# Mixers' modulation weights multiplied on POOL and summed on ACT, with inputs in one transfer, tables on POOL and the ones products reordered

## The chip, the cores and the metric

The kernel runs on one core of a Trainium2 chip. The metric is the device time of one execution in microseconds (us); of the kernel before three runs gave a median of 806.41 us (806.21 to 808.29). The engines are PE (TensorE), DVE (VectorE), ACT (ScalarE), POOL (GpSimd) and SP, whose queue issues the transfers.

## The reference

Two layers of a trunk on x (256 tokens x 1024 channels, f32), each a mixer and a convolutional FFN, both behind a modulated RMSNorm; a last RMSNorm ends it.

```python
for l in range(2):
    mod = c @ mod_w[l] + mod_b[l]                     # 1024 -> 6 x 1024
    sh1, sc1, g1, sh2, sc2, g2 = split(mod, 6)
    h = rmsnorm(x, norm1_g[l]) * (1 + sc1) + sh1
    x = x + g1 * mixer(h, positions, w_in[l], ...)    # sparse + forgetting attention, gates, w_out
    h = rmsnorm(x, norm2_g[l]) * (1 + sc2) + sh2
    x = x + g2 * conv_ffn(h, w_up[l], conv_w[l], conv_b[l], w_down[l])
return rmsnorm(x, final_g)
```

All is f32. The mixer's index branch picks the 64 best keys of each query, and both attentions have 8 heads of 64.

## The kernel before, in words

Channels lie on partitions: x is a tile of 128 x 8 x 256 (eight blocks of 128 channels, 256 tokens). To keep f32 accuracy at the speed of one pass, every weight chunk of 128 x 1024 (0.5 MB) is split into a rounded part `whi` (ACT, line 202) and the rest `wlo` (DVE, line 214, two inputs in SBUF), the activations into `hh` and `hl`, and each product is three matmuls (`mm3`, line 121).

Work is a list of steps (`add`, line 133), each with the weight chunks that it takes; `run_steps` (line 141) issues the loads on SP's queue into a ring of six slots (`RAW`), splits ahead by up to five (`SPLIT`), and calls the step. Engines named in `pin(...)` keep program order; the scheduler of the framework may reorder the others. A slot is loaded again once its last reader is done, and SP's queue keeps order.

The stages, with their place in the profiled execution: the start and the first mixer's row projection (0 to 52 us, `begin` to `go`, lines 566 to 676), the rest of mixer 0 (to 214), FFN 0 (to 405), mixer 1 (to 594), FFN 1 (to 787) and the end (`last`, `tail`, `finish`, lines 1094 to 1159).

Modulation vectors come in two ways. For layer 0's first two (shift and scale of the first norm) PE does it: `mod_mm` (line 615) multiplies chunks `wmod` by c, `mod_fin` (line 626) turns the sum, and `h_block` makes the next block of h; this runs once per block k, in front of the row products of k, with four PE transposes and small DVE steps in between. All others go through `mod_columns` (line 348): one DVE instruction per chunk of 128 x 1024 multiplies by `cB` (c broadcast) and sums (TENSOR_TENSOR_REDUCE, shown as CUSTOM_DVE_ANT_0), with the bias as its start value. There are 80: 24 in mixer 0 (`MIXV[0]`), 16 in mixer 1 and 40 in the FFNs, of which 32 are in FFN 0. In the mixers one such chunk goes with each bulk weight chunk (`bulk`, line 753).

The norms' sums go through PE: squares from ACT, partly added on DVE (`sq_add`, the first `DSUM` = 4 blocks), are multiplied by a column of ones (`sum_rows`, line 381); `rstd` (line 386) does the power on POOL, and `rstd_rows` spreads it over partitions on PE. `warm` (line 588) issues products that nobody reads, which keep PE busy while it waits there (`WARMS`).

At the start five transfers bring positions, frequencies, vectors and x (lines 245 to 250). Masks and rotary tables (`masks`, `tables`, lines 290 and 303) are 32 small, mostly DVE instructions between the squares of x.

Of the kernel before, what the change touches and what calls it, by code (L numbers as in the profile page):

```python
# [16 lines left out]
P = 128  # L17
# [22 lines left out]
WARMS = {"ffn": (4, 8, 10), "mixer": (0, 8, 7)}  # L40
# [9 lines left out]
DSUM = 4  # L50
# [15 lines left out]


@with_exitstack
def hybrid_trunk(ctx: ExitStack, tc: tile.TileContext, xT, vec, fbias, pos, invf,
# [39 lines left out]
    pad(const, 48)  # L109
# [147 lines left out]
    V.tensor_scalar(ident, jp, 0.0, None, op0=OP.is_equal)  # L257
    tri = const.tile([P, 3 * P], F32, name="tri")
    V.memset(tri[:, 0:P], 0.0)
    V.memset(tri[:, 2 * P:], 1.0)  # L260
    causal = const.tile([P, T], F32, name="causal")
    V.memset(causal[:, 0:P], 0.0)
    chunked = const.tile([P, T], F32, name="chunked")
    V.memset(chunked, 0.0)
    V.memset(chunked[0:64, P + 64:], NEG)
# [12 lines left out]
    V.tensor_copy(cpad[:, :, 0], vc[:, V_C:V_C + KT])  # L278
    cB = const.tile([P, D], F32, name="cB")
    LF = const.tile([P, 2, P], F32, name="LF")  # L280
    V.memset(LF, 0.0)
    cum = const.tile([P, T], F32R, name="cum")
    V.memset(f(cum), 0.0)
# [6 lines left out]
    def masks():  # L290
        V.tensor_scalar(tri[:, P:2 * P], jp, 0.0, None, op0=OP.is_ge)
        V.tensor_scalar(causal[:, P:], jp, 0.0, NEG, op0=OP.is_gt, op1=OP.mult)
        V.tensor_scalar(e0, ph, 0.0, -8.0, op0=OP.is_equal, op1=OP.mult)
        V.tensor_scalar(e1, ph, 32.0, -8.0, op0=OP.is_equal, op1=OP.mult)
        V.tensor_add(e2, e0, e1)
        V.tensor_copy(pick, e2)
# [6 lines left out]
    def tables():  # L303

        posf = const.tile([P, 2], F32, name="posf")
        V.tensor_copy(posf, posi)
        ang = const.tile([P, 2, 8], F32, name="ang")
        for j in range(2):
            V.tensor_scalar(ang[:, j, :], ivf, posf[:, j:j + 1], None, op0=OP.mult)
# [15 lines left out]
        V.tensor_scalar(nt, ang, PI, -TWO_PI, op0=OP.is_gt, op1=OP.mult)
        V.tensor_add(ang, ang, nt)
        V.tensor_scalar(nt, ang, -PI, TWO_PI, op0=OP.is_lt, op1=OP.mult)
        V.tensor_add(ang, ang, nt)
        V.tensor_scalar(ang, ang, 3.1415925, -3.1415925, op0=OP.min, op1=OP.max)
        A.activation(ss[:, :, 8:16], ang, AF.Sin)  # L330
        V.scalar_tensor_tensor(nt, ang, -1.0, ang, op0=OP.mult, op1=OP.min)
        V.tensor_scalar(nt, nt, PI / 2, None, op0=OP.add)
# [15 lines left out]
    def mod_columns(l, v, kind=("m",)):  # L348

        def part(n, raw):  # L350
# [6 lines left out]
            if kind[0] == "s":  # L357
                pin()
        return [((lambda raw, n=n: part(n, raw), (wmodT[COLS.index((l, v)), n], D, *kind)), None)
                for n in range(KT)]  # L360

# [203 lines left out]

    def begin():
        sq = work.tile([P, 2, 4, T], F32, name="sq0", tag="hl")
        ACC["s"] = []
# [6 lines left out]
        a, b = ACC["s"]  # L575
        V.tensor_add(a, a, b)
# [7 lines left out]
    add(tables, ahead=0)  # L584
    add(masks, ahead=0)
    HH = {}

    def warm(n):

        if n:  # L590
            t = bank("M")
        for _ in range(n):
            PE.matmul(t[:, :T], cum[:, :P], cum, start=True, stop=True)

    def mixer(l, tail=None, sums=None):
        S = {}

        def start():
            HH["h"] = work.tile([P, KT, T], F32R, name="hh"), work.tile([P, KT, T], F32R, name="hl")
            S["idx"] = [[bank("A") for _ in range(2)] for _ in range(2)]  # L600
            S["fox"] = [halves(bank("B")) for _ in range(2)]
# [12 lines left out]
        if l == 0:  # L614
# [27 lines left out]
            def go0(a, b):  # L642
                pin("V", "A", "PE")
                start()
                mod_mm(0, 0, a)
                sp = bank("C")
                sum_rows(sp, ACC["s"][0], True, True)
                mod_mm(0, 1, b)
                r = rstd(sp)
                state["split_hi"](1)  # L650
                mod_fin(0, r)
            add(go0, *mchunks[0], ahead=0)

            def go(k, w, *mc):
                hh, hl = HH["h"]
                if k == 0:
                    mod_both(1, *mc[:2])
                    mc = mc[2:]
                if k + 1 == KT:
# [3 lines left out]
                    clear_keys()  # L663
                    return
                state["split_hi"](2)
# [5 lines left out]
                if mc:  # L671
                    mod_both(k + 2, *mc)
            for k in range(KT):
                add(lambda *c, k=k: go(k, *c), (wrow[l, k], 1096, "w"),
                    *(mchunks[1] if k == 0 else ()), *(mchunks[k + 2] if k + 2 < KT else ()), ahead=0 if k + 1 < KT else None)
            add(rest)
        else:
# [7 lines left out]
            def second():  # L685
                warm(WARMS["mixer"][1])
                S["rb"] = rstd_rows(r=S["r"])
                warm(WARMS["mixer"][2])
# [19 lines left out]
            def go(k, w):  # L708
# [7 lines left out]
                if k == 1:  # L716
                    pin()
            for k in range(KT):
# [505 lines left out]
```

## Time and profile before

| | |
|---|---|
| median of 3 runs | 806.41 us (806.21 to 808.29) |
| the profiled execution, its own time | 800.14 us |
| its span, first to last instruction | 798.3 us |
| PE busy | 774.5 us (97%), 6419 matmuls |
| DVE busy | 671.2 us (84%) |
| ACT busy | 486.8 us (61%) |
| POOL busy | 8.0 us (1%) |
| DMA | 179.7 MB, 225 GB/s in the mean |

A share of the span is a mean over stages with different limits, so the view of busy time by stretch is the one to read, cut at the stages' ends. Matmuls are pipelined: a busy PE may still issue at different paces, which shows in the count of matmuls per stretch. Instructions that all go through a helper have line 88; they are told apart by their tiles.

### The profile page before, as it was taken

How to read it: one execution, taken by the hardware profiler on the slowest of the kernel's cores; microseconds unless marked ns; L12 is line 12 of the kernel's file. 1: busy time of each engine (PE TensorE's matmuls, PEld its weight loads, DVE VectorE, ACT ScalarE, POOL GpSimd, SP SyncE). 2: the span in 40 equal slices, each digit the busy share in tenths (PEclk: the TensorE clock that was granted, in tenths of full speed). 3: DMA queues.
4: the chain of work that ended last, by engine and by line, in shares of the span. 5: the costliest groups of instructions: out<-in, count | busy, mean ns of one | idle time of the engine just before them, and what ended most of it. 6: DMA issues, size and time to landing. Idle time of an engine off the chain costs nothing.

```text
span 798.3 us, 16595 instructions
## 1 busy us (share of the span) xinstructions
PE 774.5 (97%) x6419; PEld 749.7 (94%) x6419; DVE 671.2 (84%) x1441; ACT 486.8 (61%) x888; POOL 8.0 (1%) x21
## 2 busy tenths in 40 slices
PE   4999999999999999999999999999999999999996
PEld 2899989989999999999989999999999999999996
DVE  6689999998589999998776899997858887877764
ACT  4476566655386665667555756675538666666664
POOL 2000000000000000000000000000000000000000
PEclk9999999999999999999999999999999999999998
DMA  8956777888558999977534577784755766556501
GB/s 324 407 177 204 259 231 255 281 291 289 191 161 285 331 337 334 330 243 225 170 120 122 161 249 248 245 283 150 240 195 156 257 218 211 188 185 186 185 27 54
DMA packets 51919, 179.74 MB, mean 225 GB/s; under 512 B 6272, under 2 KB 6400, under 8 KB 51840
## 3 DMA queue, kind: packets, MB, share of 16 engines
q1 hardware_dynamic: 51840, 178.68, 66.5%
q8 instruction: 50, 0.82, 0.4%
q14 instruction: 29, 0.24, 0.1%
HBM read 177.61 MB, written 1.05 MB: 224 GB/s over the span
## 4 chain that ended last, share of the span: by engine, by line
PE 62%; issue 26%; DVE 8%; ACT 3%; DMA 1%; SPq 0%; POOLq 0%; POOL 0%; DVEq 0%; ACTq 0%
PE psA L88 39%; PE psB L88 19%; DVE wlo L88 2%; PE psM L88 2%; DVE sc L88 1%; PE psC L88 1%; DVE raw L88 1%; ACT whi L88 1%; DMA raw<-wqkf 1%; DMA x<-xT 1%; DVE lg L88 1%; DVE m L88 0%; ACT sq L88 0%; ACT y L88 0%; DVE x L88 0%
## 5 line engine op out<-in xcount | busy, mean ns | idle before, releaser
L88 ACT ACTIVATE whi<-raw 128x1024 fp32r<-128x1024 f32 (+3 forms) x252 | 254.3, 1013 | 140.8 <-PE psA L88 55.8
L88 DVE TENSOR_TENSOR wlo<-raw,whi 128x1024 fp32r<-128x1024 f32 (+3 forms) x252 | 292.1, 1165 | 56.3 <-ACT whi L88 55.4
L88 PE MATMUL psB<-hl,whi 128*128 128x256 f32 x768 | 212.9, 279 | 0.5 <-DVE hl L88 0.5
L88 PE MATMUL psB<-hh,whi 128*128 128x256 f32 x768 | 212.8, 279 | 0.0
L88 PE MATMUL psB<-hh,wlo 128*128 128x256 f32 x768 | 212.6, 278 | 0.0
L88 PEld LDWEIGHTS psB<-hl,whi 128*128 128x128 f32 x768 | 143.7, 188 | 1.0 <-DVE hl L88 0.9
L88 PEld LDWEIGHTS psB<-hh,wlo 128*128 128x128 f32 x768 | 144.0, 188 | 0.0
L88 PEld LDWEIGHTS psB<-hh,whi 128*128 128x128 f32 x768 | 143.6, 188 | 0.2
L88 PE MATMUL psA<-hh,whi 128*128 128x256 f32 x448 | 127.7, 286 | 0.1
L88 PE MATMUL psA<-hl,whi 128*128 128x256 f32 x448 | 125.3, 280 | 0.0
L88 PE MATMUL psA<-hh,wlo 128*128 128x256 f32 x448 | 125.0, 280 | 0.0
L88 DVE CUSTOM_DVE_ANT_0 raw<-raw,cB,vc 128x1024 f32<-128x1024 f32 x80 | 101.6, 1272 | 0.5 <-DMA raw<-wmodT 0.5
L88 PE MATMUL psA<-gl,whi 128*128 128x256 f32 x352 | 97.7, 278 | 0.0
L88 PE MATMUL psA<-gh,whi 128*128 128x256 f32 x352 | 97.4, 279 | 0.3
L88 PE MATMUL psA<-gh,wlo 128*128 128x256 f32 x352 | 97.6, 278 | 0.0
L88 PEld LDWEIGHTS psA<-hh,whi 128*128 128x128 f32 x448 | 84.0, 188 | 2.2 <-issue 1.7
L88 PEld LDWEIGHTS psA<-hl,whi 128*128 128x128 f32 x448 | 84.2, 188 | 0.4
L88 PEld LDWEIGHTS psA<-hh,wlo 128*128 128x128 f32 x448 | 84.1, 188 | 0.0
L88 DVE SCALAR_TENSOR_TENSOR y<-us,vc,y 128x255 f32<-128x255 f32 (+1 forms) x176 | 76.1, 477 | 3.8 <-ACT y L88 3.7
L88 PEld LDWEIGHTS psA<-gh,whi 128*128 128x128 f32 x352 | 65.7, 188 | 0.7 <-ACT gh L88 0.7
L88 PEld LDWEIGHTS psA<-gh,wlo 128*128 128x128 f32 x352 | 66.2, 188 | 0.0
L88 PEld LDWEIGHTS psA<-gl,whi 128*128 128x128 f32 x352 | 66.0, 188 | 0.0
(202 smaller groups left out, 1173.5 us busy)
## 6 DMA issues: line engine op xcount, KB each, us to landing
raw<-wup SPq DMA_DIRECT2D x88, 512.0 KB, 4.3
raw<-wmodT SPq DMA_DIRECT2D x80, 512.0 KB, 4.9
raw<-wdn SPq DMA_DIRECT2D x44, 512.0 KB, 3.9
raw<-wgate SPq DMA_DIRECT2D x32, 512.0 KB, 4.5
raw<-wrow SPq DMA_DIRECT2D x16, 548.0 KB, 6.5
raw<-wbr SPq DMA_DIRECT2D x16, 512.0 KB, 4.8
raw<-wout SPq DMA_DIRECT2D x16, 512.0 KB, 4.0
raw<-wqa SPq DMA_DIRECT2D x16, 320.0 KB, 2.9
```

The lines of the kernel that those rows point to most:

```text
L88: r = fn(*a, **kw)
```

## The change

POOL multiplies each of the mixers' 40 modulation chunks by `cB` in place, and ACT sums it (Identity with an accumulator); DVE adds the bias once per vector. In mixer 1 six of the 16 chunks go into the row steps k = 2 to 7. The inputs that the start needs go in front of x in one array, which two transfers bring. Constant tiles, masks and the angles of the rotary tables are made on POOL in pieces between the first row steps; `clear_keys` goes from the last row step to the start. Products that nobody reads run on PE from the start (`warm`; the old `warm` is now `idle`). The sums of squares of the two halves of x go through PE one by one, and the row products of block 0 are issued in three passes around the modulation of block 1. Chunks for `mod_mm` are taken one block ahead instead of two. `gains` of the second norm moves into the last `merge`; the split behind FFN's first blocks and the opening of its modulation loads (`epoch`) go from block 1 to block 4. At the FFNs' ends fewer squares are added on DVE (3 and 2 instead of 4), the last one's sums go between its blocks, and the result leaves in two transfers instead of four.

```diff
-WARMS = {"ffn": (4, 8, 10), "mixer": (0, 8, 7)}
+WARMS = {"ffn": (4, 8, 10), "mixer": (3, 9, 7)}
-DSUM = 4
+DSUM = (3, 2)
+NS = 96
-    pad(const, 48)
+    pad(const, 80)
-    nc.sync.dma_start(posi, pos)
-    nc.sync.dma_start(ivf, invf)
-    nc.sync.dma_start(vc[:, :V_L + V_CW], vec[:, :V_L + V_CW])
-    for i in range(2):
-        nc.sync.dma_start(x[:, 4 * i:4 * i + 4, :], xT[:, 4 * i:4 * i + 4, :])
+    nc.sync.dma_start(xs[:, :half], xT[:, :half])
+    nc.sync.dma_start(xs[:, half:], xT[:, half:])
...
-    V.memset(f(cum), 0.0)
+    G.memset(f(cum), 0.0)
...
+    def mod_products(vectors):
+        def part(l, v, n, raw):
+            raw = raw[:, :D]
+            G.tensor_tensor(raw, raw, cB, op=OP.mult)
+            A.activation(raw, raw, AF.Identity, accum_out=MOD[l][:, 8 * v + n:8 * v + n + 1])
+            if n == KT - 1:
+                o = V_L + l * V_PER + V_MODB + 8 * v
+                m = MOD[l][:, 8 * v:8 * v + 8]
+                V.tensor_tensor(m, m, vc[:, o:o + 8], op=OP.add)
...
+    def warm(n):
+        for _ in range(n):
+            PE.matmul(HD["fox"][1][:, 0, :], cum[:, :P], cum, start=True, stop=True, skip_group_check=True)
     def begin():
+        pin("V", "PE")
+        clear_keys()
+        HD["fox"] = [halves(bank("B")) for _ in range(2)]
+        HD["sp"] = bank("C")
+        warm(20)
...
+        V.tensor_scalar(ident, jp, 0.0, None, op0=OP.is_equal)
+        G.tensor_copy(cpad[:, :, 0], xs[:, V_C:V_C + KT])
+        G.tensor_copy(vc[:, :V_L + V_CW], xs[:, :V_L + V_CW])
...
-        a, b = ACC["s"]
-        V.tensor_add(a, a, b)
...
             def go0(a, b):
                 pin("V", "A", "PE")
+                sum_rows(HD["sp"], ACC["s"][0], True, False)
+                mod_mm(0, 0, a)
+                sum_rows(HD["sp"], ACC["s"][1], False, True)
+                r = rstd(HD["sp"])
+                mod_mm(0, 1, b)
+                state["split_hi"](1)
+                warm(4)
+                mod_fin(0, r)
+                warm(10)
                 start()
...
+            def first(w, a, b):
+                products(w, 0)
+                state["split_hi"](2)
+                mod_both(1, a, b)
+                products(w, 1)
+                state["split"](2)
+                mod_fin(1)
+                products(w, 2)
...
+                for fn in {0: [masks, angles], 1: [turns, clamp], 3: [tables]}.get(k, ()):
+                    add(fn, ahead=0)
...
+            late += mod_products(MIXV[l])
             for k in range(KT):
                 add(lambda w, k=k: go(k, w), (wrow[l, k], 1096, "w"), ahead=(0, 0, 1)[k] if k < 3 else None)
+                if k > 1:
+                    m, keep = late.pop(0)
+                    add(*m, keep=keep)
...
-        for v in MIXV[l]:
-            mods += mod_columns(*v)
+        mods += late
...
-                if k == 1:
+                if k == 4:
                     state["split"](4)
                     epoch(l + 1)
                     pin()
...
-                    if n < DSUM:
+                    if n < DSUM[l]:
...
+                if l + 1 == L:
+                    if b == 2:
+                        sum_rows(S["sp"], ACC["a"], True, False)
+                        pin("A", "PE")
+                    while sq and sq[0][0] < 2 * b:
+                        sums(False)
...
+            A.activation(y[:, 0, c], S["tok"][i][0], AF.Copy, scale=r[:, 0:1])
+            V.tensor_scalar(y[:, 1, c], S["tok"][i][1], r[:, 1:2], None, op0=OP.mult)
+            nc.sync.dma_start(rows[:, :, c], y[:, :, c])
```

## Rows read from the trace of the kernel before

**Rows 1.** Stretches: us; busy PE, PEld, DVE, ACT, POOL (count); clock; DMA share; GB/s.

```profile
17.60:49.90 32.30, 32.17 (x291) 27.61 (x287) 19.73 (x44) 15.19 (x23) 0.00 (x0) 1.00 0.87 337
...
88.00:180.00 92.00, 89.72 (x723) 84.02 (x722) 90.31 (x253) 58.34 (x144) 0.00 (x0) 1.00 0.80 270
...
240.00:400.00 160.00, 160.00 (x1414) 160.00 (x1413) 151.36 (x245) 102.96 (x158) 0.00 (x0) 1.00 0.82 281
...
469.00:538.00 69.00, 68.58 (x546) 64.16 (x546) 68.05 (x205) 46.40 (x119) 0.00 (x0) 1.00 0.79 265
...
640.00:780.00 140.00, 140.00 (x1191) 140.00 (x1190) 104.45 (x161) 88.22 (x133) 0.00 (x0) 1.00 0.53 170
...
5.00:17.60 12.60, 6.44 (x42) 3.21 (x42) 8.37 (x40) 5.61 (x8) 0.81 (x2) 1.00 1.02 406
...
405.00:409.10 4.10, 4.10 (x22) 3.97 (x21) 1.15 (x4) 1.10 (x3) 0.69 (x1) 0.58 0.01 4
```

**Rows 2.** Timeline of the start: start us, us, engine, line, what, idle before.

```profile
2.11 0.91 SPq L250 DMA_DIRECT2D x<-xT  x2
...
7.92 1.06 ACT L88 ACTIVATE sq<-x 128x1024 f32<-128x1024 f32 x1 [0.23 <-DMA x<-xT]
...
15.74 1.94 PE L88 MATMUL psM<-raw,cpad 128*32 128x256 f32 x16
...
17.60 0.64 PE L88 MATMUL psA<-whi,hh 128*128 128x320 f32 x1
...
21.93 1.07 PE L88 MATMUL psM<-rawg,cpad 128*32 128x256 f32 x16
...
22.93 0.54 PE L88 MATMUL psA<-whi,hh 128*128 128x320 f32 x2
```

**Rows 3.** Groups by line in 88 to 180 us: shapes, count, busy us, mean ns.

```profile
L88 DVE CUSTOM_DVE_ANT_0 raw<-raw,cB,vc 128x1024 f32<-128x1024 f32 x24 | 30.4, 1272 | 0.5 <-DMA raw<-wmodT 0.5
L88 DVE TENSOR_TENSOR wlo<-raw,whi 128x1024 fp32r<-128x1024 f32 (+1 forms) x24 | 28.8, 1200 | 0.4 <-ACT whi L88 0.4
L88 ACT ACTIVATE whi<-raw 128x1024 fp32r<-128x1024 f32 x24 | 25.4, 1060 | 22.1 <-PE psA L88 15.6 <-DMA raw<-wgate 4.8 <-DMA raw<-wqkf 1.4
...
L88 DVE TENSOR_SCALAR lg<-lg,rs 128x128 f32<-128x128 f32 (+1 forms) x32 | 8.8, 314 | 0.0
...
L88 ACT ACTIVATION_READ_ACCUMULATOR lg<-lg,nb 128x1 f32 x32 | 6.1, 192 | 0.0
```

**Rows 4.** Waits of PE over the whole span: us, times, longest.

```profile
PE psA L88 <- DVE lg L88: 2.5, 3, 1.2
```

**Rows 5.** Timeline of the start: POOL's memsets and small DVE instructions beside and behind them.

```profile
3.56 0.55 POOL L301 MEMSET kzl<- 128x512 f32 x1
...
4.18 0.47 DVE L88 CAST ri<-nt 128x16 int32<-128x16 f32 x1
...
5.38 0.17 DVE L88 CAST ri<-nh 128x16 int32<-128x16 f32 x1
```

**Rows 6.** Timeline where FFN 0 and mixer 1 begin: from the variance to h.

```profile
216.43 0.16 DVE L88 TENSOR_SCALAR var<-psC 128x2 f32<-128x2 f32 x1 [1.13 <-PE psC L88]
...
218.16 0.87 DVE L88 SCALAR_TENSOR_TENSOR ht<-x,gain,psC 128x256 f32<-128x256 f32 x2 [1.58 <-PE psC L88]
...
405.23 0.16 DVE L88 TENSOR_SCALAR var<-psC 128x2 f32<-128x2 f32 x1 [1.24 <-PE psC L88]
...
407.92 0.87 DVE L88 SCALAR_TENSOR_TENSOR ht<-x,gain,psC 128x256 f32<-128x256 f32 x2 [2.53 <-PE psC L88]
```

**Rows 7.** Timeline of the end.

```profile
787.48 0.42 DVE L88 TENSOR_TENSOR sqacc<-sqacc,sq 128x256 f32<-128x256 f32 x1 [0.48 <-ACT sq L88]
...
787.82 1.65 DVE L88 SCALAR_TENSOR_TENSOR x<-psA,mod,x 128x256 f32<-128x256 f32 x4
...
790.21 0.40 ACT L88 ACTIVATE sq<-x 128x256 f32<-128x256 f32 x1
...
793.42 1.82 SPq L1159 DMA_DIRECT2D out_dram<-yout  x4
```

More of the change, by code (lines that the diff above doesn't have):

```diff
@@ L583, in hybrid_trunk, with idle @@
     add(begin, ahead=0)
-    add(tables, ahead=0)
-    add(masks, ahead=0)
     HH = {}
-    def warm(n):
+    def idle(n):
         if n:
@@ L598, in start @@
         def start():
-            HH["h"] = work.tile([P, KT, T], F32R, name="hh"), work.tile([P, KT, T], F32R, name="hl")
+            if "sp" not in HD:
+                HH["h"] = work.tile([P, KT, T], F32R, name="hh"), work.tile([P, KT, T], F32R, name="hl")
+            HD.pop("sp", None)
             S["idx"] = [[bank("A") for _ in range(2)] for _ in range(2)]
-            S["fox"] = [halves(bank("B")) for _ in range(2)]
+            S["fox"] = HD.pop("fox", None) or [halves(bank("B")) for _ in range(2)]
+        late = []
+        if l == 0:
+            late += mod_products(MIXV[l])
         def rows(k, w, part):
@@ L643, in go0, with products @@
                 pin("V", "A", "PE")
-                start()
[L645 to L651, printed above, removed]
-            add(go0, *mchunks[0], ahead=0)
+                sum_rows(HD["sp"], ACC["s"][0], True, False)
[5 more added lines that the diff above has]
+                warm(4)
+                HH["h"] = work.tile([P, KT, T], F32R, name="hh"), work.tile([P, KT, T], F32R, name="hl")
+                mod_fin(0, r)
+                warm(10)
+                start()
+            add(go0, *mchunks[0], ahead=0)
+            def products(w, i):
+                hh, hl = HH["h"]
+                a, m = ((hh, w[0]), (hl, w[0]), (hh, w[1]))[i]
+                for j in range(2):
+                    for c, (c0, c1) in enumerate(((0, 320), (320, 584))):
+                        PE.matmul(S["idx"][j][c][:, :c1 - c0], a[:, 0, j * P:(j + 1) * P], m[:, c0:c1],
+                                  start=i == 0, stop=False)
+                for q in range(4):
+                    c = slice(584 + q * P, 584 + (q + 1) * P)
+                    PE.matmul(S["fox"][q // 2][:, q % 2, :], m[:, c], a[:, 0, :], start=i == 0 and q % 2 == 0,
+                              stop=False, skip_group_check=True)
+            def first(w, a, b):
[6 more added lines that the diff above has]
+                products(w, 2)
             def go(k, w, *mc):
                 hh, hl = HH["h"]
-                if k == 0:
-                    mod_both(1, *mc[:2])
-                    mc = mc[2:]
                 if k + 1 == KT:
@@ L670, in go @@
                 state["split"](2)
-                if mc:
-                    mod_both(k + 2, *mc)
             for k in range(KT):
-                add(lambda *c, k=k: go(k, *c), (wrow[l, k], 1096, "w"),
-                    *(mchunks[1] if k == 0 else ()), *(mchunks[k + 2] if k + 2 < KT else ()), ahead=0 if k + 1 < KT else None)
+                add((lambda *c, k=k: go(k, *c)) if k else first, (wrow[l, k], 1096, "w"),
+                    *(mchunks[k + 1] if k + 1 < KT else ()), ahead=0 if k + 1 < KT else None)
+                for fn in {0: [masks, angles], 1: [turns, clamp], 3: [tables]}.get(k, ()):
+                    add(fn, ahead=0)
             add(rest)
@@ L685, in second @@
             def second():
-                warm(WARMS["mixer"][1])
+                idle(WARMS["mixer"][1])
                 S["rb"] = rstd_rows(r=S["r"])
-                warm(WARMS["mixer"][2])
+                idle(WARMS["mixer"][2])
                 S["hs"] = h_stream(l, S["rb"], 0, *HH["h"])
@@ L960, in merge @@
                 pin(*PINL)
+                gains(l, V_N2, 32)
             b = bank("A")
@@ L979, in start @@
             S["sp"] = sp = bank("C")
-            gains(l, V_N2, 32)
-            warm(WARMS["ffn"][0])
+            idle(WARMS["ffn"][0])
             sum_rows(sp, ACC["a"], True, False)
@@ L1132, in tail @@
         def tail():
-            sum_rows(S["sp"], ACC["a"], True, False)
+            if l + 1 < L:
+                idle(WARMS["mixer"][0])
+                sum_rows(S["sp"], ACC["a"], True, False)
             while S["sq"]:
@@ L1162, in hybrid_trunk @@
     run_steps()
-_ARGS = ["xT", "vec", "fbias", "pos", "invf", "wmod0", "wmodT", "cb", "wrow", "wqa", "wvf", "wqkf", "wgate", "wbr",
+_ARGS = ["xT", "vec", "fbias", "wmod0", "wmodT", "cb", "wrow", "wqa", "wvf", "wqkf", "wgate", "wbr",
          "wout", "wup", "wdn"]
```

117 lines of the change are left out of this document (65 added, 52 removed).

## Prediction

> **What bounds the kernel now.** I read the busy time by stretch first, then PE's waits, then the timeline at the stages' edges. PE is full in every long stage: 160.00 of 160 us in FFN 0, 140.00 of 140 in FFN 1, 89.72 of 92 in the bulk of mixer 0 [rows 1]. So moving work off DVE buys nothing by itself; it can only remove waits of PE. PE's first row product comes at 17.60 us [rows 2], and behind the start its largest wait is 2.5 us in three places for a scaled attention tile (`lg`) from DVE [rows 4]. DVE is close behind PE only in the mixers' bulk: 90.31 of 92 us in mixer 0 and 68.05 of 69 in mixer 1 [rows 1]. What the change can gain lies therefore at the start, at stage entries and at the end, and what it can lose lies in the mixers' bulk.
>
> One more thing is to be seen. FFN 0 issues 1414 matmuls in 160 us, 113.2 ns each, FFN 1 1191 in 140 us, 117.5 ns, both with PE always busy and the granted clock at 1.00 [rows 1]. The same instructions run at two paces. An FFN has 44 x 24 + 22 x 24 = 1584 such products, so the pace is worth 1584 x 4.3 ns = 6.8 us per FFN. The profiled execution (800.14 us; its span of 798.3 and 1.84 around it) lies 6.27 us below the median of 806.41: about one FFN at the slower pace. I make the sum against 800.14 and carry its difference over to the median.
>
> **The start.** Two transfers in place of five put x about 2.11 - 0.75 = 1.36 us earlier on SP's queue [rows 2] (0.75: the queue's first issue in the trace, estimate). From 5 us on the DMA delivers 406 GB/s [rows 1], its fullest, so arrivals are counted in bytes: x with its front 1.1 MB, per block k 1.05 MB of `wmod` and 0.56 MB of `wrow`. Before, the second half of x is seen at 7.92 [rows 2] with 1.1 MB moved. After, block 2's `wmod`, the last thing that must land before the row products of block 1, has 1.1 + 1.05 + 0.56 + 1.05 + 0.56 + 1.05 = 5.4 MB, 4.3 MB behind x: 7.92 - 1.36 + 4.3 / 0.406 = 17.2 us. Its 16 products take 0.5 to 1.0 us, so the row products of block 1 start near 17.6, where before they start at 22.93 [rows 2]: -5.3 us. The compute chain must keep up: squares of the second half end at 7.6, two adds (0.68 and 0.42) give 8.7, the sum, the power on POOL, two PE turns and the steps to h some 3.8 us, as in the trace of before from 13.8 to 17.6 [rows 2]. That puts the first row products at 12.5, and block 1's behind them at 17.6 or a little earlier: chain and DMA come out together. A lower bound of the gain is -4.0 (1.3 us lost to POOL's queue, below), an upper one -6.0.
>
> What hides the rest: the 34 products that nobody reads lie in PE's waits; at the half pace of the start 20 of them take 20 x 0.24 = 4.8 us (half of 1.94 us per 16 is what later takes 1.07 [rows 2]) from about 2.7, just until x is squared; if they came 1 us later, that would go onto the path. POOL gets eight memsets of 0.55 us [rows 5], eight shorter ones and two copies before `mod_mm`, some 6 us from 0.7, done by 7; the power stands behind these only. The 32 mask and angle steps then have until the rotation near 47 us, also if each takes the 0.7 us of a whole `rstd`. Taking `wmod` one block ahead costs nothing after block 1: seven blocks take PE 32.3 us, 4.6 each, and the DMA 1.6 / 0.406 = 3.9 each. The two Sin with a table load, estimated at 2 us, fit into ACT's idle time there (15.19 us busy of 32.30 [rows 1], 2.4 us free per block).
>
> **Entry of mixer 1.** The clock falls there: granted 0.58 over 405 to 409.1 [rows 1], that is the 1.2 GHz level for most of it, after PE had waited for sums. From variance to h it takes 407.92 - 405.23 = 2.69 us, at FFN 0's entry, in the same instructions at 2.4 GHz, 218.16 - 216.43 = 1.73 [rows 6]. The three products before the sums may keep the clock up: -0.96. One add of 0.42 us less on DVE ahead of the last residuals gives -0.4, if ACT's squares are not late next. Between 0 and -1.4 I take -1.2.
>
> **FFN entries.** `gains` (one small DVE step) leaves the chain and the split behind block 1 no longer stands before h of blocks 2 to 4. Both queues have work there that must be done anyway: 0 to -0.8, I take -0.3 for both. The modulation loads that `epoch` opens move by three blocks, some 3 us; they are first used 8 us after that.
>
> **The end.** Without the adds (0.42 us, the last at 787.48) the four last residuals, 1.65 us from 787.82, start up to 0.8 us earlier; ACT's last square at 790.21 is late next [rows 7], and in program order it no longer stands behind a scaling of x. -0.3 to -1.3, I take -0.8. Two output transfers instead of four save issue time (1.82 us for four [rows 7]), but each waits for both engines, and the bytes are the same: 0.
>
> **The mixers' bulk, the large unknown.** Removed from DVE: 24 x 1.27 = 30.4 us in mixer 0, with their read-outs 32; all 16 in mixer 1 [rows 3]. Added on ACT: 24 sums of 1.06 + 0.19 us [rows 3] = 30 us on 58.34 of 92 [rows 1], so 88 of 92: ACT takes DVE's place as the engine next to PE. In mixer 1 six chunks leave the bulk: 46.40 + 10 x 1.25 = 59 of 69, harmless. Added on POOL: no row shows a large POOL product. Its nearest row, a memset of 512 columns in 0.55 us [rows 5], gives 1.1 us for one stream of 1024; two inputs and an output one after the other 3.3 us. I take the middle, 2.2 us: 24 x 2.2 = 53 of 92 us, POOL itself has room, and a ring slot is held some 3 us longer, against some 2.5 us that SP's loads have to spare.
>
> What a POOL product does to DVE is the point. Small DVE casts take 0.47 us while POOL's memsets run and 0.17 us behind them [rows 5]; the long ones end when a memset ends. So some DVE work waits for POOL's instruction. How much a two-input split waits for a POOL product no row shows; it lies between 0 and the whole product. The Trainium skill (SBUF — State Buffer, Who interferes with whom) says that a DVE instruction with two SBUF inputs or in a two-port mode and a POOL instruction that reads SBUF shut each other out for the whole instruction; the casts agree for one input against a writing POOL. By GPSIMD Engine Reference (3.1 Elementwise) a product of 2048 columns takes 4497 ns, so 2.25 us here, as an estimate; with both rules the sum would be the first rival's, about no change.
>
> Of DVE's remaining 58 us in mixer 0's bulk, 37.6 are splits and scalings of SBUF tiles [rows 3], in 56 instructions, and 20 us are other work, 0.4 us between two of them. A product of length d that shuts DVE out costs it d - 0.4. At half of that, 24 x 1.8 / 2 = 22 us, DVE has 80 of 92 us and is still less loaded than now. So I take a small gain: half of the 2.5 us that PE waits for `lg`, -1.3 (bounds -2.5 and the first rival's cost).
>
> **Sum.** -5.3 - 1.2 - 0.3 - 0.8 - 1.3 = -8.9 us: 791.2 against 800.14, and 797.5 against the median of 806.41.
>
> **Rivals.** *POOL shuts DVE out (slower).* DVE then has 58 + 24 (d - 0.4) us for 92; the bulk grows from d = 1.82 on, and by 24 x (d - 1.82) eats the other 7.6 us at d = 2.14. At d = 2.6 it costs 18.7: 806.4 - 7.6 + 18.7 = 817.5. Place: the 24 chunks between 88 and 180 us; mixer 1 with ten chunks has room until d = 2.6. For: the casts. Against: they met a writing instruction. Between d = 1.9 and 2.3 it ends within the measurement's reach, near 806.
> *ACT waits for POOL.* Each sum stands in ACT's queue until its product is done; at 88 of 92 us, 0.5 us of waiting per sum adds 24 x 0.5 - 4 = 8 us: again about 806. For: ACT brings `whi`, evacuates PE's banks, and keeps order. Against: the scheduler may place the sum later.
> *The pace.* The stretches between are re-cut by every move, and an FFN may fall into the other pace: 6.8 us down, 790.7. The runs of before seem to have both at the slower one.
> *It does not do what it says.* The start stays bound by the DMA's arrivals as before and by POOL's queue (only 1.4 us earlier): 801.5.
>
> **How the numbers follow.** Forecast 797.5 (793 to 802): 0.44. The pace, 784 to 793: 0.16. Start without its gain, 801.5: 0.06. POOL or ACT cost about the gain, 804 to 808.8: 0.13. POOL's lock costs more, 809 to 825: 0.21. About 0.3%, 2.4 us, is what a measurement of this kernel can tell from none. Faster 0.66, same 0.13, slower 0.21. The range leaves out the lower third of the pace case and the upper half of the lock case: 787 to 813.
>
> **What would show it.** Right: the row products of block 1 near 17.6 us, a granted clock of 1.00 around the entry of mixer 1, the last square of the end 0.8 us after PE's last product earlier than now, POOL products near 2.2 us and splits still at 1.20 us. Wrong: splits of 2 us and more beside POOL, ACT idle in front of the sums, PE waiting for `wlo` in mixer 0's bulk, or a pace of the FFNs other than 113 and 117 ns, one each.

## The result, and the profile after

The changed kernel takes 857.6 us in the median of 6 runs (856.91 to 858.6), the kernel before 806.32 beside it: a ratio of 1.0645 [1.0614, 1.0676], 6.4% slower. The prediction was 797.5, its range ended at 813, so it was wrong in sign and by 60 us. The profiled execution takes 858.31 us. From the page of the changed kernel: busy time of each engine, then groups of instructions.

```profile
PE 809.9 (95%) x6473; PEld 780.8 (91%) x6473; DVE 685.8 (80%) x1326; ACT 531.1 (62%) x968; POOL 126.2 (15%) x104
...
L381 POOL TENSOR_TENSOR raw<-raw,cB 128x1024 f32<-128x1024 f32 x40 | 105.9, 2650 | 385.5 <-DVE y L91 176.0
...
L91 ACT ACTIVATE raw<-raw 128x1024 f32<-128x1024 f32 x40 | 42.3, 1059 | 42.1 <-POOL raw L381 42.0
```

POOL's 40 products take 105.9 us, the shortest 2.35 and the median 2.41 each. I had taken 2.2. The stretch that answers to the bulk of mixer 0 [rows 1] and DVE's groups in it [rows 3]:

```profile
88.00:180.00 92.00, 75.60 (x528) 68.84 (x527) 81.68 (x171) 64.53 (x152) 49.00 (x19) 0.91 0.63 211
```

```profile
L91 DVE TENSOR_TENSOR wlo<-raw,whi 128x1024 fp32r<-128x1024 f32 (+1 forms) x19 | 30.9, 1633 | 0.1
L91 DVE TENSOR_SCALAR lg<-lg,rs 128x128 f32<-128x128 f32 (+1 forms) x24 | 14.4, 635 | 0.4
```

PE falls from 89.72 busy us and 723 matmuls to 75.60 and 528, at a mean clock of 0.91. The splits (`wlo`) grow from 1200 to 1633 ns, the scalings (`lg`) from 314 to 635: the same work, counted as busy while it waits. How a single step waits is seen in the timeline of DVE and POOL at one product (start us, us):

```profile
96.27 2.37 POOL L381 TENSOR_TENSOR raw<-raw,cB 128x1024 f32<-128x1024 f32 x1 [2.06 <-DMA raw<-wmodT]
...
96.86 1.94 DVE L91 TENSOR_SCALAR sc<-sc 128x256 f32<-128x256 f32 x1
98.72 2.35 DVE L91 TENSOR_TENSOR wlo<-raw,whi 128x1024 fp32r<-128x1024 f32 x2
100.40 2.90 POOL L381 TENSOR_TENSOR raw<-raw,cB 128x1024 f32<-128x1024 f32 x1 [1.76 <-DMA raw<-wmodT]
101.10 0.42 DVE L91 TENSOR_TENSOR cum<-psC,ch 32x256 fp32r<-32x256 f32 x1
```

A scaling of 256 columns, some 0.3 us elsewhere, takes 1.94 us and ends with the product (98.80 and 98.64). The step on `psC`, a PSUM bank, takes its 0.42 us in the middle of the next product. PE's waits, which answer to [rows 4]:

```profile
PE psA L91 <- DVE lg L91: 10.2, 7, 2.3
PE psA L91 <- ACT X L91: 8.3, 2, 4.3
```

At the end of FFN 0, where four products of mixer 1 start ahead of mixer 1's variance, the same is seen on a step of the FFN that takes 0.42 us elsewhere:

```profile
422.72 2.50 POOL L381 TENSOR_TENSOR raw<-raw,cB 128x1024 f32<-128x1024 f32 x1 [176.03 <-DVE y L91]
423.21 2.28 DVE L91 TENSOR_TENSOR y<-y 128x256 f32<-128x256 f32 x1 [0.26 <-ACT y L91]
```

Where the time goes, by stage, from the variance rows of each trace. The first column runs from the start of the span to the variance of FFN 0; each further one from one variance to the next. All are us; "POOL" is the number of products, in mixer 0 + elsewhere.

| kernel | POOL | to FFN 0 | FFN 0 | mixer 1 | FFN 1 | time |
|---|---|---|---|---|---|---|
| before | 0 | 216.4 | 188.8 | 190.6 | 195.8 | 806.3 |
| after | 24 + 16 | 245.7 | 199.2 | 209.3 | 195.3 | 857.6 |
| e1_dve_sums | 0 | 216.3 | 195.4 | 191.4 | 195.6 | 807.2 |
| e2_only_products | 24 + 16 | 247.3 | 195.4 | 212.6 | 195.6 | 854.9 |
| e3_no_product | 0 | 219.7 | 195.7 | 195.6 | 194.8 | 814.6 |
| e4_pool_writes | memsets | 219.3 | 196.0 | 193.6 | 194.8 | 812.5 |
| e5_no_sums | 24 + 16 | 243.1 | 199.0 | 209.6 | 194.8 | 855.2 |
| e10_short_products | 24 + 16 | 243.4 | 202.1 | 208.7 | 194.8 | 857.8 |
| e12_mixer1_only | 0 + 16 | 217.5 | 197.1 | 206.5 | 194.8 | 824.7 |
| e9_half | 12 + 8 | 236.5 | 199.7 | 203.4 | 188.9 | 837.3 |
| e13_half_no_sums | 12 + 8 | 222.5 | 197.1 | 197.7 | 194.8 | 821.0 |
| e14_no_work | 0 | 214.2 | 193.5 | 188.5 | 194.8 | 799.7 |
| e7_start_order | 0 | 212.1 | 196.2 | 191.6 | 189.4 | 801.9 |
| e8_late_chunks | 0 | 212.0 | 193.5 | 191.1 | 194.8 | 800.2 |
| e11_four_outputs | 0 | 211.5 | 193.5 | 191.5 | 194.8 | 799.9 |

Times are medians where a kernel was timed several times (before, after, e1, e2, e7, e8, e11), else one execution. An FFN runs at one of two paces some 6 us apart (below), so single totals are read only for what is larger; FFN 1 at 188.9 and 189.4, and FFN 0 of before and of e12_mixer1_only, ran at the faster pace.

### The profile page after: what moved, and what is told of

Read it like the earlier page. It is cut to its first block, busy times and chain, and to the rows that moved or that the text cites. A ratio compares the mean times of both kernels' runs of the same rounds, so it can differ in the third digit from the quotient of the medians.

```text
span 856.5 us, 16783 instructions
## 1 busy us (share of the span) xinstructions
PE 809.9 (95%) x6473; PEld 780.8 (91%) x6473; DVE 685.8 (80%) x1326; ACT 531.1 (62%) x968; POOL 126.2 (15%) x104
## 4 chain that ended last, share of the span: by engine, by line
PE 67%; DVE 13%; ACT 6%; DMA 5%; POOL 5%; issue 3%; POOLq 0%; SPq 0%; ACTq 0%; DVEq 0%
PE psA L91 35%; PE psB L91 29%; DVE wlo L91 6%; DMA raw<-wmodT 5%; POOL raw L381 3%; PE psM L91 2%; DVE lg L91 1%; ACT whi L91 1%; DVE sc L91 1%; ACT lg L91 1%; ACT raw L91 1%; PE psC L91 1%; DVE nb L91 1%; ACT y L91 1%; DVE y L91 1%
## 5 line engine op out<-in xcount | busy, mean ns | idle before, releaser
L91 DVE TENSOR_TENSOR wlo<-raw,whi 128x1024 fp32r<-128x1024 f32 (+3 forms) x252 | 307.4, 1225 | 66.4 <-ACT whi L91 65.4
L381 POOL TENSOR_TENSOR raw<-raw,cB 128x1024 f32<-128x1024 f32 x40 | 105.9, 2650 | 385.5 <-DVE y L91 176.0
L91 PE MATMUL psA<-hh,whi 128*128 128x256 f32 x448 | 133.0, 298 | 9.9 <-ACT X L91 8.3
L91 PE MATMUL psA<-hl,whi 128*128 128x256 f32 x448 | 130.0, 291 | 0.0
L91 PE MATMUL psA<-hh,wlo 128*128 128x256 f32 x448 | 129.6, 290 | 0.0
L91 PEld LDWEIGHTS psA<-hh,whi 128*128 128x128 f32 x448 | 89.2, 200 | 13.0 <-ACT X L91 8.8
L91 PEld LDWEIGHTS psA<-hl,whi 128*128 128x128 f32 x448 | 89.6, 200 | 0.4
L91 PEld LDWEIGHTS psA<-hh,wlo 128*128 128x128 f32 x448 | 89.3, 200 | 0.0
L91 DVE SCALAR_TENSOR_TENSOR y<-us,vc,y 128x255 f32<-128x255 f32 (+1 forms) x176 | 78.5, 490 | 2.9 <-ACT y L91 2.7
L91 ACT ACTIVATE raw<-raw 128x1024 f32<-128x1024 f32 x40 | 42.3, 1059 | 42.1 <-POOL raw L381 42.0
```

The lines of the kernel that those rows point to most:

```text
L91: r = fn(*a, **kw)
L381: G.tensor_tensor(raw, raw, cB, op=OP.mult)
```

## The experiments

**Which part makes the loss.** My theory was the lock between POOL's products and DVE, the rivals ACT's queue and the other parts of the change.

e1_dve_sums, the change without its first part:

```diff
-            G.tensor_tensor(raw, raw, cB, op=OP.mult)
-            A.activation(raw, raw, AF.Identity, accum_out=MOD[l][:, 8 * v + n:8 * v + n + 1])
...
+            o = V_L + l * V_PER + V_MODB + 8 * v + n
+            V.tensor_tensor_reduce(out=raw, in0=raw, in1=cB, op0=OP.mult, op1=OP.add, scale=1.0,
+                                   scalar=vc[:, o:o + 1], accum_out=MOD[l][:, 8 * v + n:8 * v + n + 1])
```

> The changed kernel with the mixers' 40 modulation chunks multiplied and summed in one DVE instruction again, at the places of the changed kernel; all else as changed. Theory (POOL's products shut DVE out and through it PE): the 51 us go back, 800 to 808 us, `wlo` at 1.17 us in the mean. Rival (start, row passes, idle products or DMA order cost it): 840 us or more. The start itself should stay as in the changed kernel (row products of block 1 near 23 us).

Measured 807.25, ratio 1.0016 [0.9988, 1.0044]. The whole loss is in the products and sums, and all the other parts together give nothing that these runs can tell.

e2_only_products, the reverse: the kernel before, with its `mods` taken from `mod_products`.

```diff
-        for v in MIXV[l]:
-            mods += mod_columns(*v)
+        mods += mod_products(MIXV[l])
```

> The kernel before with nothing changed but the mixers' 40 chunks: product on POOL, sum on ACT, bias on DVE once per vector. Theory: nearly the whole loss, 840 to 860 us, with the variance of FFN 0 some 25 to 30 us later than 216 us. Rival (it needs the other parts to hurt): under 815 us.

Measured 854.9, ratio 1.0585 [1.0512, 1.0658].

e3_no_product leaves POOL's multiplication out (first line), e5_no_sums ACT's sum (second line) and the bias adds (that part of the modulation is a constant):

```diff
-            G.tensor_tensor(raw, raw, cB, op=OP.mult)
```

```diff
-            A.activation(raw, raw, AF.Identity, accum_out=MOD[l][:, 8 * v + n:8 * v + n + 1])
```

> The changed kernel without POOL's multiplications; ACT sums the chunks as they are, so the modulation vectors are not the reference's. ACT's load stays. Theory (POOL against DVE): 800 to 812 us. Rival (ACT, 30 us more on it in mixer 0, is the new bound): 835 us or more.

> The changed kernel with POOL's multiplications but without ACT's sums and the bias adds; the modulation vectors are a constant, so the result is not the reference's. Theory (POOL against DVE): 840 to 858 us, POOL products 2.4 us and more, splits beside them up to 3 us. Rival (ACT): 800 to 815 us.

Measured 814.6 and 855.2. Without the products 7 us of loss against e1_dve_sums are left, and PE waits 6.0 us for `X` from ACT, whose queue holds the sums; without the sums the loss is nearly whole. The sums on ACT cost 7 us by themselves; beside the products, leaving them out gives back 2.4 us.

**The lock by itself.** e6_side_by_side is a kernel of its own; the three DVE instructions `two`, `one` and `bank`, and the loop that sets them beside POOL's products and memsets:

```python
V.tensor_tensor(o1, ra, rb, op=OP.subtract)
V.tensor_scalar(o2, ra, 2.0, None, op0=OP.mult)
V.tensor_tensor(o3[:, :512], ps, rb[:, :512], op=OP.subtract)
...
for dve, k in ((two, 12), (one, 12), (bank, 16)):
    for pl, t, m in ((product, pa, 6), (write, pm, 10)):
        pl(m)
        dve(k)
        barrier(t)
```

> A kernel of its own that leaves out the whole model: three kinds of DVE instruction (a subtraction of two SBUF tiles 128x1024, a scaling of one SBUF tile 128x1024, a subtraction that reads 512 columns of a PSUM bank and 512 of SBUF), each run alone and then beside a row of POOL products 128x1024 and beside a row of POOL memsets 128x1024. Theory (a POOL product and a DVE instruction on SBUF shut each other out for the whole instruction): beside products the two-input subtraction alternates with POOL, 2.4 us are added to some or all of them while POOL runs, whichever engine wins; the scaling of one SBUF tile likewise; the subtraction from PSUM keeps the time it has alone, within 10%. Beside memsets: the two-input subtraction keeps its time, the scaling does not. Rival A (they share the port, each at half its speed): every DVE instruction beside a product takes about 1.5 to 2 times its time alone, none the length of a product more. Rival B (any POOL instruction hinders any DVE instruction): memsets lengthen the two-input subtraction too, and the subtraction from PSUM takes longer beside products.

Its timeline: the three kinds alone, then six products alone, then each kind beside products and beside memsets (start us, us, and the count at the end of the line):

```profile
8.93 10.04 DVE L47 TENSOR_TENSOR o<-ra,rb 128x1024 f32<-128x1024 f32 x8
18.89 5.78 DVE L51 TENSOR_SCALAR o<-ra 128x1024 f32<-128x1024 f32 x8
24.58 5.76 DVE L55 TENSOR_TENSOR o<-psx,rb 128x512 f32<-128x512 f32 x8
...
30.68 14.42 POOL L64 TENSOR_TENSOR pprod<-ga,gb 128x1024 f32<-128x1024 f32 x6
...
45.49 18.73 POOL L64 TENSOR_TENSOR pprod<-ga,gb 128x1024 f32<-128x1024 f32 x6
...
45.64 27.22 DVE L47 TENSOR_TENSOR o<-ra,rb 128x1024 f32<-128x1024 f32 x12
...
73.11 10.03 POOL L68 MEMSET pmem<- 128x1024 f32 x10
...
73.28 15.08 DVE L47 TENSOR_TENSOR o<-ra,rb 128x1024 f32<-128x1024 f32 x12
...
88.77 20.84 DVE L51 TENSOR_SCALAR o<-ra 128x1024 f32<-128x1024 f32 x12
...
109.85 13.85 POOL L68 MEMSET pmem<- 128x1024 f32 x10
...
110.02 15.68 DVE L51 TENSOR_SCALAR o<-ra 128x1024 f32<-128x1024 f32 x12
...
126.12 11.56 DVE L55 TENSOR_TENSOR o<-psx,rb 128x512 f32<-128x512 f32 x16
...
140.97 11.56 DVE L55 TENSOR_TENSOR o<-psx,rb 128x512 f32<-128x512 f32 x16
```

A product alone takes 2.40 us. Twelve subtractions of SBUF tiles take 12 x 1.255 = 15.06 us alone and 27.22 beside six products: 12.16 more, 2.03 for each product. The scalings take 12 x 0.72 = 8.67 alone and 20.84 beside products, again 12.17 more. The two engines take turns: the longest subtraction and the longest scaling are each 2.05 us above the shortest (ns min/median/max).

```profile
L47 DVE TENSOR_TENSOR o<-ra,rb x32: 1217/1226/3267, 8.9 to 87.1; 128x1024 f32<-128x1024 f32 x32
L51 DVE TENSOR_SCALAR o<-ra x32: 685/1010/2735, 18.9 to 125.0; 128x1024 f32<-128x1024 f32 x32
```

Beside memsets the subtractions keep their time (15.08), while the scalings take 15.68, and the memsets 13.85 in place of 10.03. What reads a PSUM bank takes 0.72 us in all three cases. So it is an exclusive lock: DVE waits for all but 0.37 us of each product (2.40 - 2.03), and half-speed sharing and a general hindrance both fall. The Trainium skill (SBUF — State Buffer, Who interferes with whom) has this rule, for the whole instruction; the run agrees on who waits for whom in every case tried, and on the length but for the 0.37 us.

e4_pool_writes asks whether writing alone does it inside the kernel (memsets for the product, so that part of the modulation is a constant):

```diff
-            G.tensor_tensor(raw, raw, cB, op=OP.mult)
+            G.memset(raw, 1.0)
+            G.memset(raw, 0.5)
```

> The changed kernel with POOL's product of each modulation chunk left out: POOL writes the chunk twice with a constant instead (two memsets of 128x1024, some 1.1 us each by rows 5, so about the product's time), and ACT sums it. The modulation of both layers is thereby constants. Theory (a product shuts DVE's SBUF work out because it reads SBUF; a write alone shuts out one-input work only): the two-input splits keep 1.17 to 1.2 us, only the one-input scalings and casts wait, so a quarter to a half of the loss is left, 815 to 835 us. Rival (POOL's SBUF traffic of any kind shuts DVE out): as with the products, 850 us and more. Rival (only ACT's place behind POOL counts): as without products, about 815 us.

Measured 812.5, as without any product. DVE's groups of this kernel in 88 to 180 us:

```profile
L91 DVE TENSOR_TENSOR wlo<-raw,whi 128x1024 fp32r<-128x1024 f32 (+1 forms) x24 | 28.9, 1203 | 7.6 <-ACT whi L91 7.5
...
L91 DVE TENSOR_SCALAR lg<-lg,rs 128x128 f32<-128x128 f32 (+1 forms) x32 | 12.4, 455 | 0.6
```

The splits keep 1.20 us; only the one-input scalings wait (455 against 314 ns), and no cost of that wait shows in these two single runs. I had expected a quarter of the loss or more from it: wrong.

**Why 50 us and not 14.** By my budget a product of 2.41 us costs mixer 0 24 x (2.41 - 1.82) = 14 us and mixer 1 nothing. Against e1_dve_sums the table has 29 in mixer 0 and, with the end of FFN 0, 22 behind it. Four runs bear on this. e9_half and e12_mixer1_only give part of the chunks back to DVE's `tensor_tensor_reduce`, e9 behind `if n % 2:`, e12 behind `if l == 0:`. e10_short_products cuts each product into four:

```diff
-            G.tensor_tensor(raw, raw, cB, op=OP.mult)
+            for c in range(4):
+                G.tensor_tensor(raw[:, 256 * c:256 * c + 256], raw[:, 256 * c:256 * c + 256], cB[:, 256 * c:256 * c + 256], op=OP.mult)
```

> The changed kernel with every second modulation chunk multiplied on POOL and summed on ACT, the others multiplied and summed by one DVE instruction as before. Theory (a budget of DVE's time in the mixer's bulk: work left plus 2.41 - 0.4 us for each product): in mixer 0 58 + 12 x 1.27 + 12 x 2.0 = 97 us for 92, so 5 us over, mixer 1 still has room: 812 to 816 us. Rival (each product costs the path a share of its own, whatever room DVE has, because PE's next turn waits for the DVE step that it shuts out): half of the loss of 50 us, 828 to 836 us.

> The changed kernel with POOL's products and ACT's sums in mixer 1 alone (16 chunks); mixer 0's 24 are summed by DVE as before. The prediction (mixer 1 has room until a product takes 2.6 us): no loss, 807 us as in e1_dve_sums. Rival (each product stands in the way of steps that PE waits for, room or not): mixer 1 is 15 to 17 us longer, the end of FFN 0, where six of its chunks run, another 2 to 4: 822 to 829 us.

> The changed kernel with each POOL product of 1024 columns cut into four of 256, some 0.65 us each (2.41 / 4 and a fixed part). Theory (DVE loses POOL's whole time, however it is cut): 852 to 862 us. Rival (what hurts is how long one short step of DVE must wait, 2.4 us in a chain where PE waits for it): the waits of the small one-input steps fall to a quarter, DVE gets its turn between two pieces, and more than a third of the loss goes: 825 to 840 us.

Measured 837.3, 824.7 and 857.8. By stages, against e1_dve_sums, half the products cost 20.2 us in mixer 0, 4.3 in FFN 0 and 12.0 in mixer 1, 36 of the 51 us (the total shows 30, as FFN 1 ran at the faster pace); both ranges were missed, the budget's by more. Mixer 1, which I had called harmless, loses 15 us with products there alone. Pieces (from the tile's view of `cB`, ns min/median/max) help nothing in the total:

```profile
L382 POOL TENSOR_TENSOR raw<-raw,cB x160: 714/740/4508, 87.5 to 557.3; 128x256 f32<-128x256 f32 x160
```

Four pieces are 2.96 us in place of 2.41. The time is the theory's, but the way to it is another. In 88 to 180 us DVE is busy for 72.16 us, where the changed kernel has 81.68, and PE's two largest waits there are for ACT, whose sums wait for POOL:

```profile
88.00:180.00 92.00, 76.29 (x553) 69.53 (x551) 72.16 (x173) 65.47 (x157) 68.18 (x80) 0.91 0.67 220
...
PE psA L91 <- ACT X L91: 7.4, 1, 7.4
PE psA L91 <- ACT pt L91: 7.2, 4, 3.5
...
L91 ACT ACTIVATE raw<-raw 128x1024 f32<-128x1024 f32 x20 | 21.2, 1062 | 20.1 <-POOL raw L382 20.1
```

So DVE does get turns between pieces, as the rival said, but POOL is then busy for 68.18 us and ACT's sums come late. What pieces cost without the sums no run shows.

e14_no_work and e13_half_no_sums separate a full DVE from held-up steps. Neither sums anything or adds a bias (that part of the modulation is a constant); e14 leaves the multiplication out as well, e13 multiplies even chunks on POOL; the edit of e13 (e14 has none of its two last lines):

```diff
-            G.tensor_tensor(raw, raw, cB, op=OP.mult)
-            A.activation(raw, raw, AF.Identity, accum_out=MOD[l][:, 8 * v + n:8 * v + n + 1])
...
+            if n % 2 == 0:
+                G.tensor_tensor(raw, raw, cB, op=OP.mult)
```

> The changed kernel with the mixers' modulation chunks loaded but neither multiplied nor summed (that part of the modulation is a constant): the floor for the next run. DVE has 58 of 92 us of work in mixer 0's bulk, so nothing but PE should bound it: mixer 0 from its first variance to the next 205 to 207 us as with DVE's sums (207.1 in e1_dve_sums) or 1 to 2 us less, total 803 to 807 us.

> The same with POOL's product of every second chunk, and no sums: 20 products in all, 12 of them in mixer 0. Theory (a budget: what counts is DVE's own work and POOL's time together against the stage's time): 58 + 12 x 2.41 = 87 us for 92, so DVE keeps room and the loss against the run without work is 0 to 3 us. Rival (each product holds up DVE steps that PE waits for, whatever room there is): 1.0 to 1.3 us for each of 20, 20 to 26 us more than the run without work.

Measured 799.7 and 821.0: 21.3 us for 20 products. The stretch 88 to 180 us, first without work, then with twelve of the products (columns as in rows 1):

```profile
88.00:180.00 92.00, 91.94 (x742) 86.16 (x741) 70.84 (x212) 60.58 (x147) 0.00 (x0) 1.00 0.83 287
```

```profile
88.00:180.00 92.00, 85.91 (x668) 77.94 (x667) 83.00 (x199) 54.76 (x141) 28.62 (x11) 1.00 0.74 248
```

Here DVE is idle for 9 us, the clock stands at 1.00 in both, and PE still loses 6 us and 74 matmuls. PE waits for nothing there in e14; in e13 its longest wait is for a step of DVE:

```profile
PE psA L91 <- DVE lg L91: 2.5, 3, 1.1
```

So products hold up steps that PE waits for even where DVE has idle time: 8.3 us in mixer 0 for 12, 0.7 each. The other 12 (e5_no_sums) add 20.6 us, 1.7 each; by the sum DVE has no room then, 58 + 24 x 2.03 = 107 us of work and locks for 92. But the 58 may be too low: without any of this work DVE is busy for 70.84 us in e14's stretch (for 742 matmuls, where before has 723), and 70.84 + 12 x 2.03 = 95 leaves no room for e13's 12 either. So in mixer 0 a full DVE and held-up steps are not cleanly apart. Outside mixer 0 the eight products of e13 cost 3.6 in FFN 0 and 9.2 in mixer 1, 1.6 each. Five of them lie in the bulk of mixer 1, which shows in e14 so:

```profile
460.00:530.00 70.00, 69.99 (x554) 66.52 (x554) 58.37 (x201) 45.88 (x112) 0.00 (x0) 1.00 0.68 241
```

There 58.37 + 5 x 2.03 = 68.5 us fits into 70, and the products cost PE time all the same.

**The start, the entry and the end.** With the sums back on DVE the other parts can be judged, step by step. e7_start_order is e1_dve_sums with POOL's instructions of the start in program order:

```diff
-    V, A, PE, G = Engine("V", nc.vector), Engine("A", nc.scalar), Engine("PE", nc.tensor), nc.gpsimd
+    V, A, PE, G = Engine("V", nc.vector), Engine("A", nc.scalar), Engine("PE", nc.tensor), Engine("G", nc.gpsimd)
...
-        pin("V", "PE")
+        pin("V", "PE", "G")
...
-                pin("V", "A", "PE")
+                pin("V", "A", "PE", "G")
```

> The version whose chunks DVE sums again (e1_dve_sums), with POOL kept in program order at the start too, so that the power behind the first variance no longer stands behind the mask and angle steps. Theory (the start gained nothing because POOL had those steps ahead of the power): the power follows the variance (9.2 us) within 0.7 us instead of 3.8, the first row product comes near 12.5 us instead of 15.8, and the total falls by 2.5 to 5 us against 807.3, to 802 to 805. Rival (the arrival of the weights bounds the start): the first row product comes earlier, but the row products of block 1 and the end of the rows stay where they are, 50.3 us; total 807. Rival (the clock): PE at half speed until 18 us eats the gain; total 806 to 807.

Measured 801.9, ratio 0.9938 [0.9907, 0.9968]. The rows that answer to [rows 2], first of the changed kernel, then of e7_start_order: the variance, POOL's power, PE's turn with it, the first row products, those of block 1.

```profile
10.07 0.16 DVE L91 TENSOR_SCALAR var<-psC 128x2 f32<-128x2 f32 x1 [1.90 <-PE psC L91]
12.96 0.73 POOL L418 TENSOR_TENSOR rstd<-var,mhalf 128x2 f32<-128x2 f32 x1
13.74 1.22 PE L91 MATMUL psC<-ident,rstd 128*128 128x128 f32 x4 [1.12 <-POOL rstd L418]
16.90 1.18 PE L91 MATMUL psA<-whi,hh 128*128 128x320 f32 x4
23.11 0.54 PE L91 MATMUL psA<-whi,hh 128*128 128x320 f32 x2
```

```profile
9.55 0.16 DVE L91 TENSOR_SCALAR var<-psC 128x2 f32<-128x2 f32 x1 [1.54 <-PE psC L91]
9.79 0.71 POOL L91 TENSOR_TENSOR rstd<-var,mhalf 128x2 f32<-128x2 f32 x1 [2.82 <-DVE var L91]
10.85 0.61 PE L91 MATMUL psC<-ident,rstd 128*128 128x128 f32 x4
12.87 0.81 PE L91 MATMUL psA<-whi,hh 128*128 128x320 f32 x4 [0.23 <-ACT hh L91]
18.50 0.54 PE L91 MATMUL psA<-whi,hh 128*128 128x320 f32 x2
```

In the changed kernel the scheduler has put mask and angle steps ahead of the power, which starts 2.7 us after its variance is done, in e7 0.1. PE's products then run slower as well: the four with `rstd` take 1.22 us against 0.61, and the row products after them 1.18 against 0.81. The granted clock reads 1.00 there in the changed kernel, so its rows do not show the clock as the reason; in e1_dve_sums, with the same order on POOL, it is 0.50 over 16 to 18 us, after PE had waited 3.1 us for the power. In e7 both delays are gone. The end of mixer 0 comes at 212.1 us, in e1_dve_sums at 216.3.

e8_late_chunks is e7 with mixer 1's chunks out of its row steps, and e11_four_outputs is e8 with the result in four transfers of 128x512 as in the kernel before:

```diff
-                if k > 1:
-                    m, keep = late.pop(0)
-                    add(*m, keep=keep)
```

```diff
-            nc.sync.dma_start(rows[:, :, c], y[:, :, c])
+                nc.sync.dma_start(out[j * P:(j + 1) * P, c], y[:, j, c])
```

> e7_start_order with one more edit: mixer 1's modulation chunks no longer open in its row steps but all later, as in the kernel before. Theory (the entry of mixer 1 gained nothing because chunks of mixer 1 were drawn into the end of FFN 0, where they delay the last squares): no chunk's sum runs ahead of mixer 1's entry, the variance to h there takes 1.8 to 2.2 us instead of 2.96, and the total is 0.8 to 2 us under e7_start_order's. Rival (the entry is bound by the squares and by the clock that falls there anyway): the variance to h stays near 2.9 us and the totals agree within 0.5 us. Rival (the row steps were needed to spread DVE's work): DVE's chunks crowd mixer 1's bulk, 1 to 3 us more.

> e8_late_chunks with the four output transfers of the kernel before in place of two. Theory (two larger transfers are issued later, because each waits for both engines, and end later: from the variance to the end 7.0 us in every version with two, 6.66 before): 6.6 to 6.7 us from the variance to the end, the total 0.4 us under e8_late_chunks's, less than these runs can tell from none. Rival (the 0.4 us lie elsewhere in the end, such as in its scalings): still 7.0 us.

Measured 800.15 and 799.91, both a ratio of 0.9919 (intervals [0.9895, 0.9943] and [0.9895, 0.9944]): 0.8% faster than the kernel before. At the entry of mixer 1 the variance and h stand in e8 (first fence) and in e14_no_work (second) so:

```profile
405.46 0.16 DVE L91 TENSOR_SCALAR var<-psC 128x2 f32<-128x2 f32 x1 [1.29 <-PE psC L91]
...
408.03 0.87 DVE L91 SCALAR_TENSOR_TENSOR ht<-xs,gain,psC 128x256 f32<-128x256 f32 x2 [2.40 <-PE psC L91]
```

```profile
407.64 0.16 DVE L91 TENSOR_SCALAR var<-psC 128x2 f32<-128x2 f32 x1 [1.29 <-PE psC L91]
...
409.43 0.87 DVE L91 SCALAR_TENSOR_TENSOR ht<-xs,gain,psC 128x256 f32<-128x256 f32 x2 [1.63 <-PE psC L91]
```

That is 2.57 us in e8, where 1.8 to 2.2 were expected, and 2.32 in e11, against 2.96 in e1, 3.04 in e7 and 2.69 before; 1.79 in e14. The granted clock over 403 to 412 us is 0.81 in e8 and 1.00 in e14, though PE issues the same ones products ahead of the variance, 2.39 us in both. So the clock makes the difference, and what lets it fall in the one and not in the other stays open. From the last variance to the end it takes 6.66 us before, 7.03 in e8, 6.87 in e11: the two larger transfers cost 0.16 of the 0.37 us, and the rest stays open. The totals of e8 and e11 agree.

## Why the prediction was wrong, point by point

**Mixers' bulk, -1.3: the step that failed.** "At half of that" was the choice: DVE loses half of d - 0.4 per product, 0.9 us. No row gave that half. e6 shows 2.03 us at d = 2.40, the whole of d - 0.4, so that 24 products take 49 us from DVE in mixer 0 and not 22. The row I leaned on, casts beside memsets [rows 5], met a writing instruction, and e6 shows that this is another case: two-input work passes beside memsets and is shut out beside products. In place of -1.3 the products and sums cost 51 us: 29 in mixer 0, 4 in FFN 0, 18 in mixer 1. The rule of the Trainium skill (SBUF — State Buffer, Who interferes with whom), which the prediction had quoted and priced, was right, and the prediction gave a cost above 809 us 0.21. The sign "PE waiting for `wlo`" did not come: PE's waits name `lg` and ACT's `X` first, and no `wlo`.

**The rival's price was wrong too.** Even at d = 2.41 it gave about 813 us. The deduction of 0.4 us was right in size (0.37 in e6); two other terms did not hold. First, DVE's own work: with 58 us the sum is 58 + 24 x 2.03 = 107 for 92, +15, where mixer 0 lost 27 (e5) to 29; with the 70.84 of e14 it is 120, +28. Second, it was a sum of times, so that work with room to spare would cost nothing. e13 shows 1.5 us per product in mixer 1 although the sum had room, as a DVE step that PE waits for is late by up to a whole product. "Mixer 1 harmless until 2.6" fell with that: 15 us. How the loss of mixer 0 divides between the two no run isolates. A part is the clock: over 100 to 120 us and over 520 to 540 its mean grant is 0.83 in the changed kernel and 1.00 before, each time behind waits of PE. By the mean grants of the two whole spans, 0.971 of 856.5 us and 0.993 of 798.3, the lower level takes 19 us more of full-speed time than before; that is an estimate of the most it can make of the 50, and no run isolates it.

**ACT waits for POOL.** True as a mechanism (42.0 us of ACT's idle time end with a product). The sums cost 7 us without the products, and leaving them out beside whole products gains 2.4; but PE's 8.3 us of waits for `X` in the changed kernel, and its largest in e10, are for ACT while its queue holds such sums. That they are late through the products is argued, not isolated.

**The start, -5.3: came out at 0, with the right mechanism behind it.** x did come 2.1 us earlier and the variance 2.7. The step that failed is "the power stands behind these only": I took the order of the program for POOL's order, where nothing pins it. In e7 the first row products come at 12.87 (predicted 12.5) and block 1's at 18.50 (17.6), where the changed kernel has 23.11 and before 22.93: -4.4 us, inside the bounds of -4 to -6. The rival that the DMA bounds the start falls.

**Entry of mixer 1, -1.2: not reached.** In the changed kernel it takes 4.03 us, not 1.73: a product of a chunk, drawn in from the row steps, stands ahead of the power on POOL, which starts 1.8 us after its variance is done.

```profile
444.57 2.38 POOL L381 TENSOR_TENSOR raw<-raw,cB 128x1024 f32<-128x1024 f32 x1 [4.92 <-DMA raw<-wmodT]
444.93 0.16 DVE L91 TENSOR_SCALAR var<-psC 128x2 f32<-128x2 f32 x1 [1.29 <-PE psC L91]
446.90 0.69 POOL L418 TENSOR_TENSOR rstd<-var,mhalf 128x2 f32<-128x2 f32 x1
448.96 0.87 DVE L91 SCALAR_TENSOR_TENSOR ht<-xs,gain,psC 128x256 f32<-128x256 f32 x2 [3.88 <-PE psC L91]
```

In e1 it is 2.96. There a DVE sum of a chunk, 1.28 us long, stands ahead of an add of squares. Where the clock stays up it is 1.79 (e14), so the size of "-0.96" was right; but the three products alone do not keep it up (e8, e11), and that was the step.

**FFN entries, -0.3, and the end, -0.8.** The variance to h at FFN 0's entry is 1.77 us, and 1.73 before [rows 6]. FFN 1, up to the last variance, is 0.2 to 1.0 us shorter in the runs of the table at the same pace (0.2 also in e2, whose FFN is that of before); the output then gives 0.2 to 0.4 back, where I had written 0.

**The pace.** Both FFNs of the changed kernel issue at the slower pace; in 270 to 395 us 1064 matmuls in 125 us, 117.5 ns each, in 700 to 840 us 1191 in 140. FFN 0 of before has 113.2 [rows 1]. The rival's 6.8 us is seen within the runs (FFN 1 188.9 to 195.8), but both paces occur with the change and without it. What sets it stays open.

## What to carry to other kernels

Work given to POOL that reads SBUF is paid in DVE's time almost one to one (2.03 of 2.40 us), so price it as if DVE did it, at POOL's duration: here a sum of 1.27 us on DVE became a product of 2.41 us on POOL. Add what PE loses behind each held-up step. In e6 only DVE's work on a PSUM bank ran beside products undisturbed; a place in this kernel where they pay no run shows. And when steps are moved to an engine that is idle, look at what that engine must do on the critical path, and pin its place ahead of them: here the power stood once behind mask steps and once behind a product.

## What the runs showed of the hardware

A POOL product of 1024 columns and DVE work on SBUF shut each other out for all but 0.37 of 2.40 us. A product of 256 columns takes 0.74 us, more than a quarter of 2.41, and a cut into four changes nothing in the total (857.8 against 857.6). Memsets on POOL leave two-input DVE work its time (15.08 us against 15.06), and two of them per chunk in the kernel's place of the product cost nothing that shows (812.5 against 814.6 without). A one-input scaling of 0.72 us and a two-input subtraction of 1.255 lose the same 12.2 us to six products, so the faster an instruction is, the worse it fares.
